# Keys and values compressed side by side in the array, compressed scores in one pass, and value products gathered into one run

## The chip, the cores and the metric

The kernel runs on one core of a Trainium2 chip. The metric is the device time of one execution in microseconds. Three runs of the kernel before gave 1069.88, 1070.99 and 1071.37, a median of 1070.99.

## What is computed

The input is one sequence of 512 tokens, 1024 wide. The first block is an RMS norm, one wide projection, a sliding-window attention (8 heads, 2 key heads, window 128), a short gated convolution, an output projection and a gated feed-forward net of width 2816. The second block projects again and mixes three things. One is a sparse attention of 6 heads in 2 groups with three branches (compressed, selected and window) that share their queries; the others are a stick-breaking attention (4 heads) and a gated recurrence (6 heads). The parts of the reference that the change touches, cut:

```python
def compress(src, w1, w2):
    blocks = src.reshape(B, S, G, dk)[:, blk_idx] + cmp_pos[None, None, :, None, :]
    blocks = blocks.transpose(0, 3, 1, 2, 4).reshape(B, G, n_cmp, CMP_BLOCK * dk)
    return jax.nn.gelu(blocks @ w1) @ w2
kc = compress(kc_src, w_ck1, w_ck2)
vc = compress(vc_src, w_cv1, w_cv2)
...
s_c = jnp.einsum('bghtd,bgnd->bghtn', qb, kc) * scale + bias_c
p_c = masked_softmax(s_c, rel_c >= 0)
o_c = jnp.einsum('bghtn,bgnd->bghtd', p_c.astype(vc.dtype), vc)
...
return gb[..., 0:1] * o_c + gb[..., 1:2] * o_s + gb[..., 2:3] * o_w
```

Here `n_cmp` is 31 blocks per group, so 62 for both groups; a block has 32 tokens of width 64, that is 2048 numbers, or 16 slices of 128. With 512 tokens the selected branch sees every earlier block, so it is a full causal attention.

## The kernel before, in words

**Dense products.** Activations stand as 128 channels by 512 tokens. Every weight block of 1024 x 128 comes by one DMA into `raw` (2 buffers), is split into a rounded part `wh` (ScalarE, L196) and a rest `wl` (VectorE, L136 from L197), and gives 24 matmuls of 512 columns in `dense` (8 slices, three products each). The product ends in a PSUM bank (`pm`, two banks; the first four blocks of a stage alternate with `poa` and `pob`), and VectorE reads the bank (`dk<-pm,rs` and the like). Those matmuls use the type fp32r, and each is one record in the trace. A matmul of plain fp32 operands is two records there.

**The second block.** `in_proj2` goes through 33 weight blocks in the order of the table ORDER: `kc` is the third, `vc` the sixth, and the eight gates `z` end it. Beside it run three generators: `stream_a` (recurrence pairs and stick-breaking pairs, in the order of SEQ), `sparse` (the compressed branch, then 24 units of the other two branches) and `finishing`. `drive` writes them out by costs that each yields, divided by rates, and a scheduler that orders by priority and readiness makes the instruction order of each engine from that.

**The compressed branch.** `compress` (L840) is run for the keys and then for the values. It loads `w_ck1` or `w_cv1` (4 DMAs of 256 KB into `nk` buffers) and a small second weight, builds 62 blocks with VectorE adds (L857) and makes 16 fp32 matmuls (the weight slice stands still, 62 columns move), then a chain of eight small ScalarE and VectorE steps for the GELU. Small products follow: the keys `kcT` (128 x 62) and the values `vcn`. For each of 4 token blocks `compressed` then makes the scores: for each of two groups three fp32 matmuls with the query block standing still and 31 key columns moving, `pgb<-kcT,np`.

**The value products.** A unit of the sparse part (head pair j, token block i, branch br) makes scores (`nsa_a`), a softmax, transposes of the probabilities (L965), a copy of them to SBUF by VectorE for one group and ScalarE for the other (`pT`, L967), and products with the values (`pob<-nk,np`). Each product uses half the array's columns, since a group has 64 of the 128 output rows; the two groups alternate. `run` puts the products of one unit together at high priority, and they wait for the copies. The products of the compressed branch (`pob<-np,vcn`) go with branch 0. The first block's `softmax_b` works alike: 8 units, each with one run into `poa` or `pob`.

## Time and profile before

| what | value |
|---|---|
| median of 3 runs | 1070.99 us |
| the profiled execution, its own time | 1068.53 us |
| its span in the trace | 1066.8 us |
| granted TensorE clock, mean | 0.999 of 2.4 GHz |
| TensorE (PE) busy | 1039.5 us, 97% |
| VectorE (DVE) busy | 704.4 us, 66% |
| ScalarE (ACT) busy | 488.8 us, 46% |
| GpSimd (POOL) busy | 44.0 us, 4% |
| DMA | 97.84 MB, mean 92 GB/s |

The span is what the instructions cover, and 1.7 us of the execution lie around it. Busy time of PE is a modelled figure: matmuls overlap, so two records of 0.39 us can start 0.23 us apart. What a matmul costs is therefore read from where the next one starts.

### The profile page before, as it was taken

How to read it: one execution, taken by the hardware profiler on the slowest of the kernel's cores; microseconds unless marked ns; L12 is line 12 of the kernel's file. 1: busy time of each engine (PE TensorE's matmuls, PEld its weight loads, DVE VectorE, ACT ScalarE, POOL GpSimd, SP SyncE). 2: the span in 40 equal slices, each digit the busy share in tenths (PEclk: the TensorE clock that was granted, in tenths of full speed). 3: DMA queues.
4: the chain of work that ended last, by engine and by line, in shares of the span. 5: the costliest groups of instructions: out<-in, count | busy, mean ns of one | idle time of the engine just before them, and what ended most of it. 6: DMA issues, size and time to landing. Idle time of an engine off the chain costs nothing.

```text
span 1066.8 us, 14636 instructions
## 1 busy us (share of the span) xinstructions
PE 1039.5 (97%) x5712; PEld 838.9 (79%) x5712; DVE 704.4 (66%) x1313; ACT 488.8 (46%) x855; POOL 44.0 (4%) x89
## 2 busy tenths in 40 slices
PE   8999999999999999999999999999999999989997
PEld 6788888888888888888877888767777777767886
DVE  6876643356448777777763233597967698887757
ACT  5754443322344444444442222433625676578740
POOL 0000000000220000000000111200000000011000
PEclk9999999999999999999999999999999999999999
DMA  6212232333432233223335333531321110101232
GB/s 218 79 60 80 79 94 85 99 99 109 142 120 85 98 99 99 98 99 99 99 94 193 97 106 90 184 101 41 99 75 47 59 41 22 41 21 37 82 120 79
DMA packets 32801, 97.84 MB, mean 92 GB/s; under 512 B 4878, under 2 KB 5390, under 8 KB 32732
## 3 DMA queue, kind: packets, MB, share of 16 engines
q1 hardware_dynamic: 32732, 96.91, 28.7%
q8 instruction: 45, 0.74, 0.3%
q14 instruction: 24, 0.20, 0.1%
HBM read 94.77 MB, written 5.27 MB: 94 GB/s over the span
## 4 chain that ended last, share of the span: by engine, by line
PE 75%; DVE 11%; ACT 7%; DMA 3%; issue 2%; SPq 1%; POOL 1%; DVEq 0%; POOLq 0%; ACTq 0%
PE pm L139 44%; PE pob L139 12%; PE poa L139 12%; PE pga L139 4%; PE pgb L139 3%; DVE wl L136 2%; DMA raw<-in_w_in 1%; ACT wh L196 1%; DVE lv L136 1%; DMA raw<-in_w_down 1%; DVE hk L136 1%; DVE dk L136 1%; DVE np L136 1%; DVE nk L942 1%; ACT nk L948 1%
## 5 line engine op out<-in xcount | busy, mean ns | idle before, releaser
L139 PE MATMUL pm<-x,wh 128*128 128x512 f32 (+1 forms) x1360 | 433.4, 395 | 2.1 <-DVE x L133 0.9
L139 PEld LDWEIGHTS pm<-x,wh 128*128 128x128 f32 (+1 forms) x1360 | 252.2, 187 | 58.5 <-issue 3.5
L196 ACT CAST wh<-raw 128x1024 fp32r<-128x1024 f32 (+1 forms) x153 | 156.7, 1025 | 275.8 <-issue 109.9
L139 PE MATMUL pm<-x,wl 128*128 128x512 f32 (+1 forms) x680 | 268.3, 395 | 0.0
L136 DVE TENSOR_TENSOR wl<-raw,wh 128x1024 fp32r<-128x1024 f32 (+1 forms) x153 | 181.9, 1189 | 89.5 <-ACT wh L196 87.7
L139 PEld LDWEIGHTS pm<-x,wl 128*128 128x128 f32 (+1 forms) x680 | 127.0, 187 | 26.8 <-issue 1.6
L139 PE MATMUL poa<-x,wh 128*128 128x512 f32 x208 | 65.0, 394 | 0.0
L139 PE MATMUL pob<-x,wh 128*128 128x512 f32 x208 | 64.1, 390 | 0.0
L139 PE MATMUL pm<-np,wh 128*128 128x512 f32 x176 | 54.1, 389 | 0.0
L136 DVE TENSOR_TENSOR dk<-pm,rs 128x512 f32<-128x512 f32 x43 | 29.5, 686 | 28.1 <-PE pm L139 28.0
L139 PEld LDWEIGHTS poa<-x,wh 128*128 128x128 f32 x208 | 39.0, 188 | 9.3 <-issue 1.0
L139 PEld LDWEIGHTS pob<-x,wh 128*128 128x128 f32 x208 | 39.0, 188 | 8.0
L136 DVE TENSOR_TENSOR nk<-pm,rs 128x512 f32<-128x512 f32 x34 | 23.4, 687 | 32.6 <-PE pm L139 32.4
L139 PE MATMUL poa<-x,wl 128*128 128x512 f32 x104 | 40.6, 390 | 0.1
L139 PE MATMUL pob<-x,wl 128*128 128x512 f32 x104 | 40.6, 390 | 0.0
L139 PEld LDWEIGHTS pm<-np,wh 128*128 128x128 f32 x176 | 33.0, 188 | 6.8
L139 PE MATMUL pm<-np,wl 128*128 128x512 f32 x88 | 34.2, 389 | 0.0
L948 ACT ACTIVATE nk<-nk,q 128x128 f32<-128x128 f32 (+3 forms) x48 | 26.5, 555 | 11.5 <-DVE q L946 11.2
L942 DVE CUSTOM_DVE_ANT_0 nk<-pgb,bi 128x128 f32<-128x128 f32 (+3 forms) x48 | 23.1, 484 | 7.9 <-PE pgb L139 7.2
L133 DVE SCALAR_TENSOR_TENSOR dk<-nk,smt,dk 128x511 f32<-128x511 f32 (+1 forms) x34 | 25.4, 748 | 1.4 <-ACT dk L435 0.8
L139 PE MATMUL pgb<-np,np 128*128 128x128 f32 (+3 forms) x96 | 25.9, 351 | 0.4 <-DVE nk L967 0.3
L133 DVE SCALAR_TENSOR_TENSOR nk<-nk,smt,nk 128x511 f32<-128x511 f32 (+2 forms) x33 | 24.7, 747 | 0.5
(498 smaller groups left out, 1664.7 us busy)
## 6 DMA issues: line engine op xcount, KB each, us to landing
raw<-in_w_in SPq DMA_DIRECT2D x65, 512.0 KB, 3.5
raw<-in_w_up SPq DMA_DIRECT2D x44, 512.0 KB, 3.5
raw<-in_w_down SPq DMA_DIRECT2D x16, 512.0 KB, 3.6
raw<-in_w_br SPq DMA_DIRECT2D x8, 512.0 KB, 3.4
raw<-in_w_out SPq DMA_DIRECT2D x8, 512.0 KB, 3.5
raw<-in_w_out SPq DMA_DIRECT2D x16, 256.0 KB, 2.7
raw<-in_w_down SPq DMA_DIRECT2D x8, 384.0 KB, 3.2
d<-d SPq DMA_DIRECT2D x6, 512.0 KB, 6.6
```

The costliest lines, as they stand in the source:

```text
L133: V.scalar_tensor_tensor(o, i0, s, i1, op0, op1)
L136: V.tensor_tensor(o, i0, i1, op)
L139: return TE.matmul(o, l, r, start=start, stop=stop)
L196: A.copy(wh[:, c], raw[:, c])
L942: V.tensor_tensor_reduce(pb[:, 0:Wd_], s[:, 0:Wd_], bias[h][:, T - Wd_:T], 1.0, -3e38, ALU.add, ALU.max, st[:, g:g + 1])
L948: A.activation(pbs[g][:, 0:Wd_], pbs[g][:, 0:Wd_], AF.Exp, bias=st[:, 2 + g:3 + g], accum_out=st[:, 4 + g:5 + g])
```

## The change

Four things are changed.

1. `compress` becomes `blocks`, which only loads weights and builds blocks, for keys and then for values, and `compressed` makes the products of both together. The blocks now stand still (64 columns at a time, two of them unused) and the weights move (128 columns). Keys write output rows 0 to 63 and values 64 to 127 of one bank, 32 fp32 products in one `run`. The GELU chain is made once, 128 x 128, and one transpose turns its result. The `w1` tiles, blocks and the chain come from `np` in place of `nk` buffers, and both values' and keys' loads are issued ahead.
2. The keys are kept as a rounded part and a rest side by side (`kc2`, 62 columns, fp32r). The scores of a token block are 6 fp32r products of 62 columns into one bank, and VectorE adds the two halves and the bias.
3. `nsa_b` keeps its transposes and copies, and `nsa_c` makes the products of both branches of a token block in one run. In the first block `softmax_c` does so for the two units of a head pair.
4. Buffers move: the probabilities of the first block to `lv`, some gates from `lv` to `hk` and `np`, three merged tiles from `np` to `lv`.

```diff
     def small(w):
-        return qp.tile([P, w], F32, tag=f"q{w}", name=nm("q"), bufs={6: 1, 8: 4, 20: 4, 32: 2, 192: 2, 64: 5}.get(w, 6))
+        return qp.tile([P, w], F32, tag=f"q{w}", name=nm("q"), bufs={6: 1, 8: 4, 20: 4, 32: 2, 192: 2, 64: 2}.get(w, 6))
...
                 j = n - 18
                 t = scaled(ps, rstd1)
-                g = tl("bi" if j < 6 else "lv" if j < 12 else "hk" if j < 15 else "np")
+                g = tl("bi" if j < 6 else "hk" if j < 9 else "np")
...
-    def softmax_b(j, ip, po, sbs, lo):
...
-            pT = wk()
+            pT = tl("lv")
             c = slice(lo[0], T)
...
@@ -508,28 +516,33 @@
             i = 2 * ip + u
             bs = list(range(lo[u] // P, 2))
             for b in bs:
-                sblk = i + b - 1
                 for hh in range(2):
-                    r = 64 * hh
-                    todo.append(later(po[r:r + 64, i * P:(i + 1) * P], vn[:, sblk * P + r:sblk * P + r + 64],
-                                      pts[hh][:, (2 * u + b) * P:(2 * u + b + 1) * P], b == bs[0], b == bs[-1]))
-        run(todo, ends)
-        yield 1.0
+                    todo.append((i, i + b - 1, hh, pts[hh][:, (2 * u + b) * P:(2 * u + b + 1) * P], b == bs[0], b == bs[-1]))
+        return todo, ends
+
+    def softmax_c(po, held):
+        todo = []
+        for i, sblk, hh, w, first, last in held[0][0] + held[1][0]:
+            r = 64 * hh
+            todo.append(later(po[r:r + 64, i * P:(i + 1) * P], vn[:, sblk * P + r:sblk * P + r + 64], w, first, last))
+        run(todo, held[0][1] + held[1][1])
+        yield 2.0
...
             new = softmax_a(*un) if un else None
             yield 1.7
             if prev:
                 (j, ip), args = prev
-                if ip == 0:
+                held.append((yield from softmax_b(j, ip, *args)))
+                if ip == 1:
                     po = bank("oa" if j % 2 == 0 else "ob")
-                yield from softmax_b(j, ip, po, *args)
-                if ip == 1:
+                    yield from softmax_c(po, held)
+                    held = []
                     attn[j] = split(po, None, rt)
...
-            merged[j] = split(ms[0], 0.5, of("np" if j < 5 else "gp"))
...
-    def compress(name, w1name, w2name):
-        w1 = [nk().rearrange("p (k h) -> p k h", k=4) for _ in range(4)]
+    def blocks(name, w1name, w2name):
+
+        w1 = [np_().rearrange("p (k h) -> p k h", k=4) for _ in range(4)]
         for n in range(4):
             nc.sync.dma_start(w1[n], a[w1name][:, 4 * n:4 * n + 4])
         w2 = small(64)
         nc.sync.dma_start(w2, a[w2name])
         yield from need(name)
         src = pr[name]
-        blks = [nk(), nk()]
+        blks = [np_(), np_()]
         pos = S("pos").rearrange("p (r j) -> p r j", r=2)
         for n in range(2):
+            G.memset(blks[n][:, 496:512], 0.0)
             blk = blks[n][:, 0:496].rearrange("p (j n) -> p j n", j=8)
             for g in range(2):
                 s = src[64 * g:64 * g + 64]
                 for par in range(2):
                     v = bass.AP(tensor=s.tensor, offset=s.offset + par + 16 * n,
                                 ap=[list(s.ap[0]), [2, 8], [16, 31]])
-                    V.tensor_tensor(
+                    last = V.tensor_tensor(
                         blk[64 * par:64 * par + 64, :, 31 * g:31 * g + 31], v,
                         pos[64 * g:64 * g + 64, par, 8 * n:8 * n + 8].unsqueeze(2).to_broadcast([64, 8, 31]), ALU.add,
                     )
         yield 0
-        ps = bank("gb")
-        for k in range(16):
-            mm(ps[:, 0:62], w1[k // 4][:, k % 4], blks[k // 8][:, 62 * (k % 8):62 * (k % 8) + 62], k == 0, k == 15)
-        x, y = small(64), small(64)
-        A.copy(x[:, :62], ps[:, 0:62])
-        tt(y[:, :62], x[:, :62], x[:, :62], ALU.mult)
-        V.tensor_scalar(y[:, :62], y[:, :62], 0.044715, 1.0, ALU.mult, ALU.add)
-        tt(y[:, :62], y[:, :62], x[:, :62], ALU.mult)
-        V.tensor_scalar(y[:, :62], y[:, :62], -2.0 * math.sqrt(2.0 / math.pi), 80.0, ALU.mult, ALU.min)
-        A.activation(y[:, :62], y[:, :62], AF.Exp)
-        V.tensor_scalar(y[:, :62], y[:, :62], 1.0, None, ALU.add)
-        V.reciprocal(y[:, :62], y[:, :62])
-        tt(y[:, :62], y[:, :62], x[:, :62], ALU.mult)
-        pr[w1name] = y, w2
-        yield 2.0
-
-    kcT = cp.tile([P, 2, 32], F32, tag="kcT", name="kcT")
+        return w1, w2, blks, last
+
+
+    kc2 = cp.tile([P, 2, 64], F32R, tag="kc2", name="kc2")
     vcn = [cp.tile([P, 2, 64], F32, tag=f"vcn{h}", name=f"vcn{h}") for h in range(3)]
...
-        yield from compress("kc", "w_ck1", "w_ck2")
-        y, w2 = pr["w_ck1"]
+        wk1, wk2, bk, e0 = yield from blocks("kc", "w_ck1", "w_ck2")
+        wv1, wv2, bv, e1 = yield from blocks("vc", "w_cv1", "w_cv2")
+
+        ps = bank("gb")
+        todo = []
+        for k in range(16):
+            c = slice(62 * (k % 8), 62 * (k % 8) + 64)
+            for r, w1, blks in ((0, wk1, bk), (64, wv1, bv)):
+                todo.append(later(ps[r:r + 64, 0:P], blks[k // 8][:, c], w1[k // 4][:, k % 4], k == 0, k == 15))
+        run(todo, [e0, e1])
+        xy = np_()
+        x, y, yT = (xy[:, P * n:P * n + P] for n in range(3))
+        A.copy(x, ps[:, 0:P])
+        tt(y, x, x, ALU.mult)
+        V.tensor_scalar(y, y, 0.044715, 1.0, ALU.mult, ALU.add)
+        tt(y, y, x, ALU.mult)
+        V.tensor_scalar(y, y, -2.0 * math.sqrt(2.0 / math.pi), 80.0, ALU.mult, ALU.min)
+        A.activation(y, y, AF.Exp)
+        V.tensor_scalar(y, y, 1.0, None, ALU.add)
+        V.reciprocal(y, y)
+        tt(y, y, x, ALU.mult)
+        yield 2.0
+        ps = bank("gb")
+        TE.transpose(ps[:, 0:P], y, ident)
+        A.copy(yT, ps[:, 0:P])
         ps = bank("gb")
         for g in range(2):
             for r in (0, 64):
-                mm(ps[r:r + 64, 32 * g:32 * g + 31], w2, y[:, 31 * g:31 * g + 31])
-        A.copy(kcT[:, :, 0:31], ps[:, 0:64].rearrange("p (g n) -> p g n", g=2)[:, :, 0:31])
+                mm(ps[r:r + 64, 32 * g:32 * g + 31], wk2, yT[:, 31 * g:31 * g + 31])
+        kv = ps[:, 0:64].rearrange("p (g n) -> p g n", g=2)[:, :, 0:31]
+        A.copy(kc2[:, :, 0:31], kv)
+        tt(kc2[:, :, 31:62], kv, kc2[:, :, 0:31].bitcast(F32), ALU.subtract)
         yield 0.3
-        yield from compress("vc", "w_cv1", "w_cv2")
-        y, w2 = pr["w_cv1"]
         ps = bank("gb")
         for g in range(2):
             for h in range(3):
-                mm(ps[32 * h:32 * h + 31, 64 * g:64 * g + 64], y[:, 31 * g:31 * g + 31], w2)
+                mm(ps[32 * h:32 * h + 31, 64 * g:64 * g + 64], yT[:, 64 + 31 * g:64 + 31 * g + 31], wv2)
         for h in range(3):
             A.copy(vcn[h][32 * h:32 * h + 31], ps[32 * h:32 * h + 31, 0:128])
         yield 0.5
...
             pv = pc.rearrange("p (h n) -> p h n", n=32)[:, :, 0:31]
             st = small(16)
+            ps = bank("gb")
             for g in range(2):
-                ps = bank("gb")
                 for h in range(3):
-                    mm(ps[:, 32 * h:32 * h + 31], pr["nq", h][g][:, i * P:(i + 1) * P].bitcast(F32), kcT[:, g, 0:31])
-                tt(pv[:, 3 * g:3 * g + 3], ps[:, 0:96].rearrange("p (h n) -> p h n", n=32)[:, :, 0:31],
-                   biasc[i][:, 3 * g:3 * g + 3], ALU.add)
+                    n = 64 * (3 * g + h)
+                    mm(ps[:, n:n + 62], pr["nq", h][g][:, i * P:(i + 1) * P], kc2[:, g, 0:62])
+            sv = ps[:, 0:384].rearrange("p (h n) -> p h n", h=6)
+            tt(pv, sv[:, :, 0:31], biasc[i], ALU.add)
+            tt(pv, pv, sv[:, :, 31:62], ALU.add)
...
-    def nsa_b(j, i, br, po, pbs):
+    def nsa_b(j, i, br, pbs):
+
         Wd_ = (i + 1) * P
-        vn_ = pr[("vs", "vw")[br]]
         pts, ends = [], []
         for g in range(2):
             ps = bank("gb")
@@ -967,24 +994,31 @@
             ends.append((V.tensor_copy if g == 0 else A.copy)(pT[:, 0:Wd_], ps[:, 0:Wd_]))
             pts.append(pT)
         yield 0.25 * (i + 1)
-        todo = []
+        return pts, ends
+
+    def nsa_c(j, i, po, held):
+
+        todo, ends = [], []
         for g in range(2):
-            if br == 0:
-                todo.append(later(po[64 * g:64 * g + 64, i * P:(i + 1) * P], vcn[j][0:96, g],
-                                  pcT[i][0:96, g], True, False))
-        for b in range(i + 1):
-            for g in range(2):
-                r = 64 * g
-                todo.append(later(po[r:r + 64, i * P:(i + 1) * P], vn_[:, b * P + r:b * P + r + 64],
-                                  pts[g][:, b * P:(b + 1) * P], False, br == 1 and b == i))
+            todo.append(later(po[64 * g:64 * g + 64, i * P:(i + 1) * P], vcn[j][0:96, g],
+                              pcT[i][0:96, g], True, False))
+        for br, (pts, e) in enumerate(held):
+            vn_ = pr[("vs", "vw")[br]]
+            ends += e
+            for b in range(i + 1):
+                for g in range(2):
+                    r = 64 * g
+                    todo.append(later(po[r:r + 64, i * P:(i + 1) * P], vn_[:, b * P + r:b * P + r + 64],
+                                      pts[g][:, b * P:(b + 1) * P], False, br == 1 and b == i))
         run(todo, ends)
-        yield 0.16 * (i + 1)
+        yield 0.32 * (i + 1)
...
-                yield from paced(nsa_b(j, i, br, po, pbs), rate)
+                held.append((yield from paced2(nsa_b(j, i, br, pbs), rate)))
+                if br == 1:
+                    yield from paced(nsa_c(j, i, po, held), rate)
+                    held = []
```

Three places show how the order of the instructions moves. All are on PE. First the products of the compression: the keys' before, in `pgb_5297`, where `x4` is four matmuls of one weight tile (`pob_5341` is the dense product they interrupt).

```order
L139 MATMUL pob_5341<-x_4698,wh_5257 128x512
L139 MATMUL pgb_5297<-nk_5287,nk_5151 128x62 x4
L139 MATMUL pgb_5297<-nk_5287,nk_5152 128x62 x4
L139 MATMUL pob_5341<-x_4697,wl_5258 128x512
L139 MATMUL pob_5341<-x_4790,wh_5257 128x512
```

And now, where keys (`np_5151` and on) and values (`np_5299` and on) alternate in `pgb_5680`, behind the value products of a recurrence pair (`poa_5548`):

```order
L139 MATMUL poa_5548<-hk_5537,gp_5342 64x128
L139 MATMUL pgb_5680<-np_5300,np_5668 64x128
L139 MATMUL pgb_5680<-np_5152,np_5287 64x128
L139 MATMUL pgb_5680<-np_5300,np_5668 64x128
L139 MATMUL pgb_5680<-np_5152,np_5287 64x128
L139 MATMUL pgb_5680<-np_5300,np_5668 64x128
L139 MATMUL pgb_5680<-np_5153,np_5288 64x128
L139 MATMUL pgb_5680<-np_5301,np_5669 64x128
```

Four pieces of eight matmuls, each among full-array work, became 32 matmuls in three pieces (6, 5 and 21) with 64 output rows each; the last two stand on either side of that recurrence run.

Second, the value products of head pair 0, token block 1, in the first of its two branches, before (`vcn` is the compressed branch, `np_6029` the values of the selected one):

```order
L139 MATMUL pm_7730<-x_4790,wl_7415 128x512
L139 MATMUL pob_6661<-np_6550,vcn_5082 64x128 x2
L139 MATMUL pob_6661<-nk_6664,np_6029 64x128
L139 MATMUL pob_6661<-nk_6668,np_6029 64x128
L139 MATMUL pgb_6680<-np_5987,np_5782 128x256
L139 MATMUL pgb_6680<-np_5989,np_5782 128x256
```

And now, with the window branch's products (`np_6429`) in the same run:

```order
L139 MATMUL pm_7776<-x_5059,wl_7456 128x512
L139 MATMUL pob_6652<-np_6544,vcn_5082 64x128 x2
L139 MATMUL pob_6652<-nk_6655,np_6024 64x128
L139 MATMUL pob_6652<-nk_6659,np_6024 64x128
L139 MATMUL pob_6652<-nk_6681,np_6429 64x128
L139 MATMUL pob_6652<-nk_6685,np_6429 64x128
L139 MATMUL pgb_6694<-np_5936,np_5776 128x256
```

The second run of the pair is gone as a piece of its own. Counted over the whole order, stretches of matmuls on 64 output columns went from 37 to 22, and stretches on the full array from 51 to 34.

Third, the end of the last dense block that comes before six gate blocks are left. Before, from its last row on (`pm_8245`), 84 matmuls stand ahead of the next dense one:

```order
L139 MATMUL pm_8245<-x_5059,wl_8170 128x512
L139 MATMUL pob_7783<-nk_7849,np_6434 64x128
L139 MATMUL pob_7783<-nk_7853,np_6434 64x128
L139 MATMUL pgb_7869<-np_5942,np_5903 128x256
L139 MATMUL pgb_7869<-np_5944,np_5903 128x256
```

Now the same block (`pm_8266`) ends while head pair 1 is in work, and the third recurrence pair (`lv_7558`) comes behind it:

```order
L139 MATMUL pm_8266<-x_5059,wl_8195 128x512
L992 MATMUL pgb_7400<-cst,nk_7120 128x128 x4
L992 MATMUL pgb_7407<-cst,nk_7125 128x128 x4
L139 MATMUL pgb_7474<-np_5936,np_5897 128x128
L139 MATMUL pgb_7474<-np_5938,np_5897 128x128
```

284 matmuls now stand ahead of the next dense one, all of the third recurrence pair's products among them. Before, that pair stood ahead of the dense block's end.

## Rows read from the trace of the kernel before

**Rows 1.** The page: busy time, share of the span, instructions.
```profile
PE 1039.5 (97%) x5712; PEld 838.9 (79%) x5712; DVE 704.4 (66%) x1313; ACT 488.8 (46%) x855; POOL 44.0 (4%) x89
```

**Rows 2.** Timeline of PE at the keys' compression: start, us, engine, line, tiles, records.
```profile
700.01 2.00 PE L139 MATMUL pgb<-nk,nk 128*128 128x62 f32 x16 [0.35 <-DVE nk L857]
701.82 0.71 PE L139 MATMUL pob<-x,wh 128*128 128x512 f32 x2
```

**Rows 3.** Timeline of PE, two runs of value products and their neighbours.
```profile
941.56 0.40 PE L139 MATMUL pm<-x,wl 128*128 128x512 f32 x1
941.88 0.44 PE L139 MATMUL pob<-nk,np 128*64 128x128 f32 x4
942.25 0.50 PE L139 MATMUL pgb<-np,np 128*128 128x256 f32 x2
...
983.68 0.39 PE L139 MATMUL pm<-x,wl 128*128 128x512 f32 x1
983.91 0.39 PE L139 MATMUL pm<-x,wh 128*128 128x512 f32 x1
984.23 0.44 PE L139 MATMUL pob<-np,vcn 96*64 96x128 f32 x4
984.50 1.05 PE L139 MATMUL pob<-nk,np 128*64 128x128 f32 x16
985.47 0.50 PE L139 MATMUL pm<-x,wh 128*128 128x512 f32 x1
```

**Rows 4.** Waits of PE from 679 to 740 us: total, times, longest.
```profile
PE pgb L139 <- DVE nk L857: 1.3, 2, 1.0
PE pgb L139 <- issue: 0.8, 1, 0.8
```

**Rows 5.** Timeline of PE at the compressed scores, and fp32r products of 128 columns.
```profile
840.07 0.75 PE L139 MATMUL pgb<-kcT,np 128*128 128x31 f32 x6
840.66 0.71 PE L139 MATMUL pm<-x,wh 128*128 128x512 f32 x2
...
1009.92 0.61 PE L139 MATMUL pga<-trir,x 128*128 128x128 f32 x4
1010.37 0.39 PE L139 MATMUL poa<-trir,x 128*128 128x128 f32 x2
```

**Rows 6.** Waits of PE from 895 to 1005 us, the longest one.
```profile
PE pob L139 <- ACT nk L967: 1.6, 3, 0.8
```

**Rows 7.** Chain that ended last, 640 to 760 us: start, us, what.
```profile
658.60 14.74 PE pob L139 x65
673.45 6.29 DMA raw<-in_w_in
...
680.91 1.23 DVE wl L136
```

**Rows 8.** Timeline of PE, the first product of that third block.
```profile
686.28 0.62 PE L139 MATMUL pm<-x,wh 128*128 128x512 f32 x2
```

**Rows 9.** Timeline of SP: the loads ahead of that block and behind it.
```profile
670.65 2.70 SPq L821 DMA_DIRECT2D bi<-d  x6
...
676.12 2.26 SPq L843 DMA_DIRECT2D nk<-in_w_ck  x4
```

**Rows 10.** Busy time in stretches: us; PE, PEld, DVE, ACT, POOL; clock; DMA.
```profile
869.20:907.70 38.50, 37.97 (x422) 29.28 (x423) 34.34 (x114) 24.97 (x67) 1.61 (x5) 1.00 0.07 21
907.70:959.70 52.00, 48.23 (x384) 35.28 (x382) 43.56 (x138) 32.34 (x84) 2.70 (x6) 1.00 0.10 31
959.70:1008.60 48.90, 47.11 (x286) 37.63 (x286) 36.90 (x62) 39.43 (x70) 4.34 (x11) 1.00 0.17 50
```

**Rows 11.** Timeline of DVE: two reads of dense banks, one after the other.
```profile
908.00 0.68 DVE L136 TENSOR_TENSOR dk<-pm,rs 128x512 f32<-128x512 f32 x1
...
959.99 0.68 DVE L136 TENSOR_TENSOR dk<-pm,rs 128x512 f32<-128x512 f32 x1
```

**Rows 12.** Busy time in the stretch without dense work, columns as above.
```profile
941.30:960.50 19.20, 15.79 (x107) 10.69 (x105) 16.94 (x55) 14.92 (x39) 3.46 (x8) 1.00 0.09 28
```

More of the change, by code (lines that the diff above doesn't have):

```diff
@@ L162, in paced, with paced2 @@
         for c in g:
+            yield c if c is None else c / rate
+    def paced2(g, rate):
+        while True:
+            try:
+                c = next(g)
+            except StopIteration as e:
+                return e.value
             yield c if c is None else c / rate
@@ L491, in softmax_a, with softmax_b @@
         return sbs, lo
-    def softmax_b(j, ip, po, sbs, lo):
+    def softmax_b(j, ip, sbs, lo):
         pts, ends = [], []
@@ L521, in attention @@
         units = [(j, ip) for j in range(4) for ip in range(2)]
-        po = None
+        held = []
         prev = None
@@ L557, in branches @@
             tt(ms[0], ms[0], ms[1], ALU.add)
-            merged[j] = split(ms[0], 0.5, of("np" if j < 5 else "gp"))
+            merged[j] = split(ms[0], 0.5, of("np" if j < 2 else "lv" if j < 5 else "gp"))
     drive((branches(), 1.0))
@@ L680, in tile_net @@
     A.copy(trir[:, 2], ident)
-    dk, hk, nk = of("dk"), of("hk"), of("nk")
+    dk, hk, nk, np_ = of("dk"), of("hk"), of("nk"), of("np")
     def pairs(t):
@@ L987, in sparse @@
         po = None
+        held = []
         for un in [(j, i, br) for j in range(3) for i in range(4) for br in range(2)] + [None]:
@@ L995, in sparse @@
                     po = bank("ob")
-                yield from paced(nsa_b(j, i, br, po, pbs), rate)
+                held.append((yield from paced2(nsa_b(j, i, br, pbs), rate)))
+                if br == 1:
+                    yield from paced(nsa_c(j, i, po, held), rate)
+                    held = []
                 if (i, br) == (3, 1):
```

## The prediction

> **What bounds the kernel now.** I began with the page's busy times. TensorE is busy 97% of the span, VectorE 66% and ScalarE 46% [rows 1]. So a matmul saved is worth its own time, as long as the engine then finds other work. Two more views are needed. The timeline of PE, read from one start to the next, prices the matmuls that change [rows 2, 3, 5]: the reader should divide the distance to the next row's start by the number of records, since the lengths printed overlap. The busy times of stretches show where PE is not the limit. From 869 to 1009 us it has 133.3 us of work in 139.4 us (the three stretches summed), while VectorE and ScalarE have 114.8 and 96.7 [rows 10]. In the one long stretch without dense products, 941.3 to 960.5, PE is busy 15.8 of 19.2 us and VectorE 16.9 [rows 12]. There a saved matmul is not yet a saved microsecond.
>
> **The change part by part.** The sum is made against the profiled execution's own time, 1068.53 us, which is 2.5 us under the median of the runs.
>
> *Compression.* Before, the keys' first eight products are 16 records from 700.01 to 701.82, 0.113 us each [rows 2]. Both compressions have 64 records, so 7.2 us. After, there are 32 products, again 64 records, on half the columns and with 128 columns moving. The trace has that form in the value products. A run of 4 records takes 0.37 us to the next start and one of 20 records 1.24 [rows 3], so 16 more records cost 0.87, or 0.054 each. 64 of them are 3.5 us: a saving of **3.7**. It needs the two halves to work at the same time; if they didn't, a record would cost about what the full array's does, and the saving would be 0.
>
> *Waits at the compression.* Four pieces among full-array work waited 2.1 us on the block adds L857 and on issue [rows 4]. The adds remain, but one gathered run behind a recurrence run, further back in the order, needs them. I take **1.0** saved, between 0 and 2.1. The extra transpose is one record, 0.1 us more. The GELU chain is made once in place of twice. In the order 29 dense products, 6.6 us, stand between it and the transpose. That hides its eight steps of 128 columns even at the 0.68 us that 512 columns take on VectorE, 5.4 us [rows 11]; without them all of that would show.
>
> *Scores.* Six records take 0.59 us [rows 5], and there are eight such groups, 4.7 us. After, there are 24 fp32r products of 62 columns, which the trace does not show. The nearest row is fp32r with 128 columns, four records in 0.45 us, 0.11 each [rows 5], that is 2.6 us. The upper bound is two records of 0.11, 5.3 us, which would cost 0.6; the lower is half the nearest row, 1.3 us. I take 0.11, the nearest row, and a saving of **2.1** (-0.6 to 3.4). VectorE's eight adds of bias become eight of twice the width; dense work lies beside them.
>
> *Gathered runs.* A run on half columns costs something at its ends. Into it, the start of the next matmul comes 0.32 us after a 512-column one in place of 0.23, and the run of 4 records takes 0.37 where 4 times 0.054 are 0.21 [rows 3]. Together that is 0.25 us per run. The order has 37 stretches of this kind before and 22 after, 4 fewer in the first block, 12 fewer in the sparse part and one more for the compression. 15 times 0.25 gives **3.8**, with bounds of 3 and 4.5. A run also waits for the copies of the probabilities, 1.6 us in three visible waits [rows 6]. Half as many runs wait, but each for the later of two branches' copies: I take **0.5**, between 0 and 1.6.
>
> *Loads.* SP issues in order. Before, the four `w_ck1` loads left at 676.1, behind the table of biases (670.7) and the third weight block, issued at 673.45 [rows 7, 9]. Now they and two of `w_cv1`, 1.5 MB, stand ahead of the biases, two of them ahead of the second weight block. They wait for `np` buffers that the last product of the feed-forward net reads as slices 8 to 16 of 22, so from about 664 to 670 in its 14.7 us from 658.6 [rows 7]. Before, biases and third block, 2 MB, took 9.1 us from 670.65 to 679.7, and 1.5 MB are 6.8 us at that pace. Some 5 of them fit ahead of the biases. The block's split ended at 682.1 and its first product came at 686.3, 4.1 us of slack [rows 7, 8], so that some 2 us of lateness would not show. I take 0.5 us lost, between 0 and 3.
>
> *The stretch without dense work.* This term is the least sure. VectorE reads one dense bank at 908.0 and the next at 960.0 [rows 11]; in the order 136 of its instructions lie from one read to the other, now 176. In the stretch ahead (from 869.2) they go from 112 to 83, in the one behind (to 1008.6) from 61 to 49, so that the total stays (309 and 308). Before, one was busy 0.316 us on average there (43.56 us for 138 [rows 10]); 176 are 55.6 us. At the share of before, 84%, the middle takes 66 us, 14 more. The first part falls by some 6: its 210 matmuls need 32 us at the spacings above. The last falls by some 8: 138 dense products at 0.23 are 32 us, the rest 9. I take **0**. The ends are 10 us gained (VectorE never idle in the middle) and 8 lost (VectorE at 75%, its share in the last stretch of rows 10).
>
> The sum is -3.7 - 1.0 + 0.1 - 2.1 - 3.8 - 0.5 + 0.5 + 0 = **-10.5 us**: 1058.0 for the profiled execution, 1060.5 for the median. Moving buffers in the first block I cost at nothing: the gates wait for no one there, dense products lie beside them, and if a gate waited for its buffer VectorE would hold up a bank for one block, 5.4 us at most.
>
> **The rivals.** *VectorE sets the middle stretch.* For it: 284 matmuls now stand without a dense one where 84 did, with the recurrence and two sparse head pairs asking for VectorE at once. Against it: two independent chains fill each other's waits. The middle then takes 70 to 74 us in place of 66, and 4 to 8 of the 10.5 are given back: 1064.5 to 1068.5.
>
> *The halves don't work at once.* The row says they do: 0.054 us a record against 0.113 on the full array [rows 2, 3], but there each half has its own values and probabilities in a run of at most 20 records. Without it the compression saves nothing and the sum is -6.8, 1064.2. The Trainium skill, TensorE: Matmul & The Clock Gate, section "Part 3: Packing small matmuls — row/col tiling", has a weight load overlap a running matmul only where the row group differs, and here all products use all rows. By that rule the loads would stand between the products and this rival would hold; the trace disagrees, since the value products come at 0.054 us.
>
> *The scores keep two records.* If the product of 62 columns cost what fp32 did, the change would not do what it says there: the sum is -7.8, 1063.2. Against it: every fp32r matmul in the trace is one record.
>
> *The weight blocks come late.* If none of the 1.5 MB is through before the biases leave, the third block is 6.8 us late, 2.7 more than its slack, and the 0.5 of the sum becomes 2.7: 1062.7. For it: the buffers come free one after the other, and the second weight block stands behind two of them.
>
> *Slower than before.* The middle stretch is the place again, with ScalarE and VectorE waiting for each other down one chain: recurrence, then stick-breaking, then the gate blocks that wait for its `dk` buffers. It decides when VectorE's share there falls under 72%: 55.6 us of work then take 77 us, 11 more than the forecast. At 65% it is 85.5 us, and the median 1080. Against it: the share was 84% with fewer chains, and 88% without dense work [rows 12].
>
> **How the numbers follow.** The forecast gets 0.61, VectorE in the middle 0.19, the halves 0.05, the scores 0.05, the late weights 0.05 and slower 0.05. All but the last are faster by over 0.2% (2.1 us, about what a measurement of this kernel can tell from no change), except the upper edge of the second, which I give 0.04, and half of the last, 0.02, which ends within 0.2%. So faster 0.91, same 0.06, slower 0.03. The forecast's own terms range from about -16 (waits at their good ends, -2.2, and a third of the gain in the middle, -3.3) to -7 (waits, loads and scores at their bad ends). The range goes from 1054.5 to 1068: it takes in those bounds, and all rivals but the slower one and the edge.
>
> **What would show it.** In the profile of the changed kernel, `pgb<-np,np 64x128` should stand at 0.054 us a record, 64 of them; `pgb<-kc,np` at one record each, 0.11 us; 12 runs into `pob` and one run per head pair in the first block, each with its entry of 0.32 us. The stretch from the last dense product before the six gate blocks to the next should take 40 to 45 us, the middle between the two reads of VectorE about 66. The forecast is wrong if that middle takes over 74 us, if PE waits for `wh` or `wl` near 685 us, or if the compression's records are 0.1 us apart.

## The result, and the profile after

The changed kernel takes 1080.63 us (four runs, 1078.16 to 1082.20), the kernel before 1070.76: a ratio of 1.0098 with a 95% interval of 1.0084 to 1.0112. It is slower, by 9.9 us, where 10.5 less were forecast. Its profiled execution took 1078.16 us, 9.6 more than that of before.

The page, busy times and granted clock in 40 slices; against [rows 1] little has moved:
```profile
PE 1038.7 (96%) x5689; PEld 841.3 (78%) x5689; DVE 705.2 (66%) x1307; ACT 488.1 (45%) x854; POOL 45.9 (4%) x93
...
PEclk9999999999999999999999999999999999789999
```
TensorE has as much busy time as before, although 23 records are gone. The second line gives a reason: in two of the 40 slices (35 and 36, 915 to 969 us) the granted clock was well under full, which it was in no slice before (0.999 in the mean, now 0.989).

To see where the time went I counted the 512-column products on weight blocks in both traces (3576 each, 24 to a block) and noted when the same product starts, from the first weight block's end on (there the changed kernel is 0.5 us ahead). Blocks are counted from 0, and a stretch begins and ends at the last product of the block named. The table gives what each stretch gained or lost, in us:

| stretch (weight blocks) | forecast | after |
|---|---|---|
| first block's attention (1 to 30) | -1.0 | -1.4 |
| feed-forward net and its start (30 to 116) | 0 | -0.7 |
| loads (116 to 118) | +0.5 | +0.5 |
| compression (118 to 129) | -4.4 | +0.4 |
| scores, sparse part, middle (129 to 148) | -5.6 | +11.5 |
| end | 0 | -0.2 |

Two stretches failed, and they failed in waits, not in the price of a matmul. The timeline of PE in the changed kernel:
```profile
677.84 1.12 PE L139 MATMUL pgb<-nk,ones 128*128 128x512 f32 x2 [1.37 <-POOL nk L302]
...
699.42 0.66 PE L385 MATMUL pga<-cst,dk 128*128 128x128 f32 x4 [2.71 <-DVE dk L136]
699.83 0.71 PE L139 MATMUL pm<-x,wh 128*18 128x512 f32 x2
700.38 0.40 PE L139 MATMUL pm<-x,wl 128*18 128x512 f32 x1
...
726.07 0.88 PE L139 MATMUL pgb<-np,np 128*64 128x128 f32 x12 [1.10 <-ACT hk L1222]
726.88 0.71 PE L139 MATMUL pga<-lv 64*128 64x128 f32 x8
727.52 0.87 PE L139 MATMUL pgb<-np,np 128*64 128x128 f32 x10
728.38 2.40 PE L139 MATMUL poa<-hk,gp 128*64 128x128 f32 x40
730.61 2.57 PE L139 MATMUL pgb<-np,np 128*64 128x128 f32 x42
733.11 1.12 PE L139 MATMUL pga<-hk,cst 128*128 128x512 f32 x2
...
830.99 0.83 PE L139 MATMUL pgb<-kc,np 128*128 128x62 f32 x6
831.66 0.36 PE L139 MATMUL pga<-gp,np 128*128 128x256 f32 x1
...
916.51 0.45 PE L139 MATMUL pm<-x,wl 128*128 128x512 f32 x1
918.56 1.09 PE L992 MATMUL pgb<-cst,nk 128*128 128x128 f32 x8 [1.61 <-DVE nk L982]
...
921.10 3.63 PE L139 MATMUL pob<-nk,np 128*64 128x128 f32 x32
924.66 0.69 PE L139 MATMUL pgb<-np,np 128*128 128x128 f32 x2
...
975.13 0.73 PE L139 MATMUL pm<-x,wh 128*128 128x512 f32 x2
...
981.33 1.92 PE L139 MATMUL pob<-nk,np 128*64 128x128 f32 x32
983.17 0.44 PE L139 MATMUL pga<-hk,trir 128*128 128x384 f32 x1
```
The 64 records of the compression stand in three pieces, 0.81, 0.86 and 2.50 us to the next start: 0.065 each, entries included, against 0.113 in [rows 2]. Six scores take 0.67 us, 0.11 each, as taken from [rows 5]. But no dense product starts between 916.51 and 975.13, 58.6 us, where the stretch of [rows 12] had 19. And in it a run of 32 records takes 3.56 us to the next start; a run of the same form takes 1.84 at 981.33, where the clock was full.

The windows of the changed kernel (columns as in [rows 10]: busy time of PE, PEld, DVE, ACT, POOL; then the granted clock):
```profile
893.58:974.40 80.82, 69.75 (x606) 53.25 (x605) 57.80 (x179) 40.26 (x108) 2.91 (x8) 0.87 0.06 21
916.90:975.10 58.20, 46.98 (x450) 35.92 (x449) 41.74 (x121) 30.86 (x80) 2.91 (x8) 0.82 0.03 10
...
915.00:930.00 15.00, 12.88 (x210) 10.58 (x208) 10.41 (x35) 6.02 (x17) 0.00 (x0) 0.77 0.11 36
930.00:945.00 15.00, 11.00 (x71) 7.65 (x70) 11.78 (x39) 4.88 (x17) 0.00 (x0) 0.77 0.00 1
...
960.00:975.00 15.00, 13.42 (x77) 10.45 (x77) 9.95 (x24) 10.58 (x25) 2.25 (x7) 0.77 0.00 1
```
VectorE's timeline has the two reads of dense banks that bound the first window:
```profile
893.58 0.68 DVE L136 TENSOR_TENSOR dk<-pm,rs 128x512 f32<-128x512 f32 x1
...
974.40 0.68 DVE L136 TENSOR_TENSOR dk<-pm,rs 128x512 f32<-128x512 f32 x1
```
The stretch between these reads was 52.0 us in [rows 11] and is now 80.8. VectorE does there what was counted (179 instructions and 57.8 us; 176 and 55.6 were forecast), but it is busy 72% of it and not 84%. The clock of 0.82 in the long stretch is a mixture of the two levels: 0.50 of 2.4 GHz in three pieces of 6.8 to 6.9 us (from 919.5, 933.2 and 960.5 us on), each at the end of a wait of PE or just behind it, and full in between.

PE's waits in the two stretches (690 to 760, and 918 to 975 us): total, times, longest:
```profile
PE pga L385 <- DVE dk L136: 2.7, 1, 2.7
PE pga L139 <- DVE hk L1211: 1.4, 1, 1.4
PE pm L139 <- DVE dk L133: 1.3, 1, 1.3
PE pgb L139 <- ACT hk L1222: 1.1, 1, 1.1
...
PE pgb L139 <- DVE nk L994: 3.1, 4, 1.9
PE pga L139 <- ACT hk L1076: 2.5, 1, 2.5
PE pgb L992 <- DVE nk L982: 1.8, 2, 1.6
```
The first four, 6.5 us, are new at the compression; those of [rows 4], 2.1 us, are gone. VectorE's timeline at the longest:
```profile
695.12 2.92 DVE L872 TENSOR_TENSOR np<-nk,smt 64x248 f32<-64x248 f32 x5
698.08 0.69 DVE L136 TENSOR_TENSOR hk<-gp 128x512 f32<-128x512 f32 x1
698.69 0.68 DVE L136 TENSOR_TENSOR dk<-pob,rs 128x512 f32<-128x512 f32 x1
```
The read of the bank that the transposes at 699.42 need stands behind five block adds (2.92 us) and a step of the recurrence. VectorE is busy 29.8 of the 30 us from 690 to 720 there; it was 28.8 before. PE comes to this place sooner, since the keys' products are no longer here, and then waits.

### The profile page after: what moved, and what is told of

The parts are those of the page before. It is cut to its first block, busy times and chain, and to the rows that moved or that the text cites. A ratio compares the mean times of both kernels' runs of the same rounds, so it can differ in the third digit from the quotient of the medians.

```text
span 1076.5 us, 14582 instructions
## 1 busy us (share of the span) xinstructions
PE 1038.7 (96%) x5689; PEld 841.3 (78%) x5689; DVE 705.2 (66%) x1307; ACT 488.1 (45%) x854; POOL 45.9 (4%) x93
## 4 chain that ended last, share of the span: by engine, by line
PE 75%; DVE 12%; ACT 8%; DMA 2%; issue 2%; POOL 1%; SPq 1%; POOLq 0%; DVEq 0%; ACTq 0%
PE pm L139 43%; PE pob L139 12%; PE poa L139 12%; PE pga L139 3%; PE pgb L139 3%; DVE wl L136 2%; DVE hk L136 1%; DVE lv L136 1%; ACT wh L204 1%; ACT nk L975 1%; DVE dk L136 1%; DMA raw<-in_w_down 1%; DVE dk L133 1%; DVE np L136 1%; PE pgb L992 1%
## 5 line engine op out<-in xcount | busy, mean ns | idle before, releaser
L139 PE MATMUL pm<-np,wh 128*128 128x512 f32 x152 | 46.8, 389 | 0.0
L136 DVE TENSOR_TENSOR dk<-pm,rs 128x512 f32<-128x512 f32 x42 | 28.8, 686 | 23.3 <-PE pm L139 23.2
L139 PE MATMUL pgb<-np,np 128*64 128x128 f32 (+4 forms) x160 | 30.6, 329 | 4.9 <-DVE nk L994 2.8
L139 PEld LDWEIGHTS pm<-np,wh 128*128 128x128 f32 x152 | 28.5, 188 | 6.0
L139 PEld LDWEIGHTS pgb<-np,np 128*128 128x128 f32 (+1 forms) x160 | 20.1, 176 | 13.1 <-DVE nk L994 4.2
L139 PE MATMUL pm<-np,wl 128*128 128x512 f32 x76 | 29.6, 389 | 0.0
L133 DVE SCALAR_TENSOR_TENSOR nk<-nk,smt,nk 128x511 f32<-128x511 f32 (+2 forms) x33 | 24.7, 747 | 1.3 <-ACT nk L443 0.8
```

The costliest lines, as they stand in the source:

```text
L133: V.scalar_tensor_tensor(o, i0, s, i1, op0, op1)
L136: V.tensor_tensor(o, i0, i1, op)
L139: return TE.matmul(o, l, r, start=start, stop=stop)
```

## The experiments

The theories: the instruction order that the planner (`drive` and the scheduler behind it) makes from the costs (**order**); probabilities held longer for a gathered run (**buffers**); VectorE at the compression (**VectorE**); the half clock behind waits (**clock**). All are compared with the kernel before on the same chip, 1068.9 to 1069.1 us there.

**1 and 2: the planner's cost.** The change drops a cost with the second compression: two of `yield 2.0` became one.

```diff
         tt(y, y, x, ALU.mult)
-        yield 2.0
+        yield 4.0
```


> The changed kernel with one number changed: the step that ends the compression tells the planner a cost of 4.0 in place of 2.0, as the two compressions before told together. No instruction is added or removed. Order theory (the lower cost brought the sparse work about 6 us of planned time forward, which left the third recurrence pair, the second stick-breaking pair and two sparse head pairs without dense products beside them): the stretch of 284 matmuls without a dense one falls to 82, the 16 us that were lost from 900 to 990 us come back, the granted clock there is 1.00 again, and the time is 1060 to 1065 us. Buffer theory (four probability tiles held for a gathered run keep the sparse chain waiting): 1076 us or more, since the tiles are held as before. VectorE theory (it has too much work in the middle whatever the order): 1074 us or more.

The second puts the lower total into the kernel before:
```diff
         pr[w1name] = y, w2
-        yield 2.0
+        yield 1.0
```


> The kernel before with one number changed: each of its two compressions tells the planner 1.0 in place of 2.0, so that the total is 2.0 lower, as in the changed kernel. Nothing else of the change is in it. Order theory: in its instruction order a stretch of 75 and one of 190 matmuls follow each other with almost no dense product between them, so it loses 10 to 20 us: 1081 to 1091 us, with a lower granted clock in the middle. Buffer theory and the theory that gathered runs are the cause: 1069 to 1073 us, no change.

Measured: 1069.08 us for the first (ratio 0.9997, 0.9983 to 1.0011, where the changed kernel has 1.0098); 1084.10 for the second (1.0132, 1.0114 to 1.0150), 15 over the kernel before, from a number that adds no instruction. VectorE's reads of two dense banks, one after the other, in the first:
```profile
903.88 0.68 DVE L136 TENSOR_TENSOR dk<-pm,rs 128x512 f32<-128x512 f32 x1
957.50 0.68 DVE L136 TENSOR_TENSOR dk<-pm,rs 128x512 f32<-128x512 f32 x1
```
and in the second:
```profile
900.64 0.69 DVE L136 TENSOR_TENSOR dk<-pm,rs 128x512 f32<-128x512 f32 x1 [0.98 <-PE pm L139]
978.50 0.68 DVE L136 TENSOR_TENSOR dk<-pm,rs 128x512 f32<-128x512 f32 x1
```
53.6 and 77.9 us, against 52.0 before and 80.8 after. The order theory holds: the middle is lost by the cost alone, and neither held buffers nor gathered runs are needed for it. But the first run is 4 us over its range, and its clock was not full in the middle as expected (half from 945.7 to 949.1 and from 955.9 to 959.3 us). Its 12 executions spread from 1064.57 us at a mean clock of 0.995 to 1072.17 at 0.986, 0.8 us per thousandth, and its timeline of PE shows why:
```profile
699.89 1.12 PE L385 MATMUL pga<-cst,dk 128*128 128x128 f32 x4 [2.71 <-DVE dk L136]
700.66 1.20 PE L139 MATMUL pm<-x,wh 128*18 128x512 f32 x2
701.66 0.63 PE L139 MATMUL pm<-x,wl 128*18 128x512 f32 x1
```
It is the wait of the changed kernel to the hundredth, but here the products behind it stand 0.77 and 1.00 us apart where it was 0.41 and 0.55: the granted clock was half from 699.9 to 703.3 us, and full at this place in the changed kernel's profile. The Trainium skill, TensorE: Matmul & The Clock Gate, "Part 1: The HAM clock gate", has the low clock as the default that activity lifts. These rows agree, with the addition that an equal wait costs the clock in one execution and not in another.

**3, 4 and 5: one part undone.** On the first run's kernel: old compressions (3), sparse value products per branch (4), both (5). The core of each:
```diff
-        wk1, wk2, bk, e0 = yield from blocks("kc", "w_ck1", "w_ck2")
-        wv1, wv2, bv, e1 = yield from blocks("vc", "w_cv1", "w_cv2")
+        yield from compress("kc", "w_ck1", "w_ck2")
...
-                held.append((yield from paced2(nsa_b(j, i, br, pbs), rate)))
-                if br == 1:
-                    yield from paced(nsa_c(j, i, po, held), rate)
+                yield from paced(nsa_b(j, i, br, po, pbs), rate)
```


> The kernel of the first run with the two old compressions, one after the other on the full array, in place of the joint one (scores, gathered runs and buffers of the change stay). The prediction's price: 64 records at 0.113 against 0.054 us and 1.0 of waits, so 4.7 us slower than the first run. VectorE theory (from 690 to 725 us VectorE is busy without a break in both kernels and PE waits for it, so a matmul saved there only becomes a wait): at most 1.5 us slower than the first run.

> The kernel of the first run with the value products of the sparse part written out per branch as before: 12 more half-column runs, and no tiles held from one branch to the next. The prediction's price: 12 times 0.25 us and 0.5 of waits, 3.5 us slower than the first run. Theory that a gathered run gives this back by waiting for both branches' copies: within 1 us of the first run. Buffer theory: faster than the first run.

> The kernel of the first run (cost 4.0) with both the old compressions and the value products of the sparse part per branch as before; what is left of the change is the scores in one pass, the gathered runs of the first block and the buffers. Against the third run it undoes the gathered runs alone. The prediction's price of a gathered run: 3.5 us slower than the third run (1067). Theory that a gathered run, in this instruction order, gives back in the middle what it saves: 1060 to 1064, at or under the third run. Against the fourth run it undoes the joint compression alone: 4.7 us slower by the prediction's price, within 1.5 us by the VectorE theory.

Measured: 1063.37 (0.9944, 0.9927 to 0.9961), 1063.55 (0.9941, 0.9924 to 0.9958) and **1061.17 us** (0.9921, 0.9904 to 0.9938), with 1060.64 to 1061.93 in six runs. Undoing a part makes it faster, by 5.5 us and more, which no theory's range had for the third and only the buffer theory for the fourth. With the runs ungathered, the joint compression costs 2.4 us (4 against 5), outside the 1.5 that the VectorE theory allowed. Its 3 us of records come to nothing, as that theory says; the mean clock was 0.995 against 0.998 in the median, and at 0.8 us a thousandth that is an estimate of 2.4 us. The gathered runs cost 2.2 us (3 against 5). By the count of dense products, blocks 129 to 148 gain 3.3 us with gathered runs (3) and 5.3 without (5). Their waits of PE, 860 to 1010 us, in the third:
```profile
PE pga L139 <- ACT hk L1066: 2.3, 3, 1.1
PE pga L139 <- DVE hk L136: 0.9, 3, 0.5
PE pga L139 <- DVE lv L136: 0.7, 2, 0.4
```
and in the fourth:
```profile
PE poa L139 <- POOL hk L1035: 1.3, 1, 1.3
PE pob L139 <- ACT nk L994: 1.0, 3, 0.4
```
The longest waits of the third are those of stick-breaking for its chain (L1066), and the fourth and fifth have none of 0.2 us or more. In the third's order scores stand there in doubles; in the fifth's a branch's products stand between them. But the kernel before has 1.4 us of the same wait without gathering, so gathering alone does not make it. Whether the held tiles or the planner put them so was not separated.

**6, 7 and 9: the keys' adds on GpSimd**, on the kernels of runs 1, 4 and 5:
```diff
-                    last = V.tensor_tensor(
+                    last = (G if name == "kc" else V).tensor_tensor(
```


> The kernel of the first run with the eight block adds of the keys on GpSimd in place of VectorE. VectorE theory: the read of the next dense bank and the recurrence's steps no longer stand behind 4.7 us of adds, PE's wait of 2.9 us near 697 us goes and with it the half clock that followed it; 2 to 6 us faster than the first run (1063 to 1067) and less spread. If the wait of 2.9 us stays or moves to GpSimd's adds, the theory is wrong: 1068 to 1070, no change.

> The joint compression with the keys' block adds on GpSimd, the value products of the sparse part per branch, cost 4.0: the parts that each run so far speaks for. VectorE theory: faster than the fourth run by 2 to 4 us, 1059 to 1062, the fastest so far. Otherwise as the fourth run, 1063.

> The kernel of the fifth run with the eight block adds of the keys on GpSimd. VectorE theory: PE's waits at the old compression, 2.1 us in the kernel before, stand behind the adds on VectorE too, so some 1 to 2 us faster than the fifth run, 1059 to 1060, and the fastest of all. If GpSimd's adds take longer than VectorE's and the compression waits for them, 1061 or more.

Measured: 1064.68 (4.4 less than run 1), 1061.72 (1.8 less than run 4) and 1069.16 us (8.0 more than run 5). The ranges of the sixth and seventh held (the seventh was not the fastest), but the row that was to show the sixth's cause does not: the wait of 2.9 us is still there.
```profile
699.67 1.11 PE L385 MATMUL pga<-cst,dk 128*128 128x128 f32 x4 [2.95 <-DVE dk L136]
```
Other steps of the recurrence took the place of the adds ahead of that read. And while GpSimd's adds ran (690.93 to 699.59 us) VectorE's steps took longer; its timeline there:
```profile
695.19 2.96 DVE L136 TENSOR_TENSOR hk<-gp 128x512 f32<-128x512 f32 x3
```
One such step took 0.69 us in the changed kernel (698.08 above), so three end to end would take some 1.9. With three other steps in that time VectorE lost 2.4 us by the same comparison, most of the wait that stayed. So the row doesn't tell whether the adds alone held the read back before. What went is the waits further on (1.5, 1.3 and 1.1 us in run 1, on L1211, L133 and L1222), and the order had moved with the edit: the 64 records of the compression stand in one piece.
```profile
727.92 3.71 PE L139 MATMUL pgb<-np,np 128*64 128x128 f32 x64 [0.16 <-issue]
```
Which part of the 4.4 us is the adds and which the order was not separated. The ninth shows the price: GpSimd and then PE:
```profile
691.63 7.79 POOL L870 TENSOR_TENSOR nk<-nk,smt 64x248 f32<-64x248 f32 x8 [12.31 <-DVE nk L136]
...
695.92 3.00 PE L139 MATMUL pgb<-nk,nk 128*128 128x62 f32 x16 [3.28 <-POOL nk L870]
```
An add takes 0.97 us there and 0.58 on VectorE. The old compression needs them at once and waits 3.28 us, and its 16 records are busy 3.00 us where [rows 2] has 2.00: the clock fell again behind the wait (half from 696.7 to 706.9 us). The joint one of run 6 does not start before 727.9 us, well behind them.

**8: the scores alone.** Run 5 with the old scores, so that only the first block's runs and the buffers are left of the change.
```diff
-                    mm(ps[:, n:n + 62], pr["nq", h][g][:, i * P:(i + 1) * P], kc2[:, g, 0:62])
+                    mm(ps[:, 32 * h:32 * h + 31], pr["nq", h][g][:, i * P:(i + 1) * P].bitcast(F32), kcT[:, g, 0:31])
```


> The kernel of the fifth run with the old scores (48 fp32 records in eight groups, each group with a bank of its own): what is left of the change is the gathered runs of the first block and the moved buffers. The prediction's prices: the scores 2.1 us (so 1063.3, 2.1 over the fifth run) and four runs at 0.25 us (so 1.0 under the kernel before, 1068). If the scores are worth more than their records, because one bank per token block in place of two lets the dense products run on, it is 4 us or more over the fifth run.

Measured: 1067.55 us (0.9986, 0.9972 to 1.0000). The first block's runs and the buffers are worth 1.3 us, near the 1.0 forecast, with an interval that reaches from 0 to 3.0. The scores are worth 6.4, three times their records. The two profiled executions are 9.3 us apart. In the count of dense products 5.3 of these lie in blocks 129 to 148, where run 8 equals the kernel before and has its waits on stick-breaking too, and 3.4 at the compression, where the clock of run 8's execution fell to half (727.6 to 734.5 us). Why the scores move the middle was not tried further.

**10, 11 and 12: work in the waits.** Products whose result nobody reads, ahead of transposes that overwrite their bank: 12 on runs 1 and 7, of which 9 stand at the wait of 2.7 us and 3 at 572 us; 40 in the changed kernel, 35 of them in the long stretch.
```diff
     def to_nat(src, dst, tag="ga", fill=0):
         ps = bank(tag)
+        for _ in range(fill):
+            mm(ps, trir[:, 2], x2[0][0])
```


> The kernel of the first run with 12 dense-sized products more, whose result nobody reads: they write the bank that the next transposes overwrite, and in the order 9 of them stand where PE waited 2.9 us near 697 us, 3 earlier (0.7 us of added work). Clock theory (the half clock of 5 us behind that wait comes from PE's idleness in it): the granted clock from 698 to 706 us stays at 1.00, PE no longer idles there, and the transposes start when they did; the median falls by 0.5 to 2 us, to 1067 to 1068.5. If the clock falls there as before, or the products push the transposes back, the median rises by 1 to 3 us.

> The kernel of the seventh run with the same 12 products. Clock theory: the runs at a mean clock of 0.992 to 0.995 (1061.7 to 1063.5 us) go over to those at 0.998 (1059.5), so a median of 1060 to 1061. Otherwise 1061.7 to 1064.5.

> The changed kernel itself (cost 2.0, the stretch of 284 matmuls without a dense one) with 40 products of 512 columns more in that stretch and right behind it, whose result nobody reads: for each sparse unit from the last one of head pair 1 on, up to 4 stand ahead of the first transposes of its probabilities, in the bank that these overwrite. That is 9 us of added work. Clock theory (most of what the long stretch loses, about 8 us, is the half clock that PE's waits bring, at 0.84 us for each thousandth of the mean clock as the first run's executions show): the granted clock from 915 to 990 us stays nearer 1.00 than the 0.89 before, and the time does not rise although 9 us of work are added: 1074 to 1080 us. Chain theory (the stretch is as long as the chain through VectorE and ScalarE, and the clock is a bystander): the products that stand ahead of the transposes push the chain back, 1082 to 1089 us, or fit into the waits, 1080 to 1082.

Measured: 1065.67 (3.4 less than run 1, with 12 products more), 1061.52 (as run 7; its spread falls from 4.1 to 1.8 us) and 1080.17 us (1.0092, 1.0069 to 1.0115, where the changed kernel has 1.0098, with 40 products more). The tenth fell by more than its range, the eleventh lies between its two. In run 10, on the timeline of PE:
```profile
695.84 2.26 PE L139 MATMUL pga<-x,trir 128*128 128x512 f32 x9
700.13 0.66 PE L387 MATMUL pga<-cst,dk 128*128 128x128 f32 x4 [2.03 <-DVE dk L136]
```
The nine are through before the wait ends, 2.03 us remain, and in this execution the clock still fell behind it. The median clock, 0.9945 against 0.991, is higher. But the order moved with the added products: the compression's 64 records stand in one piece, as in run 6, and the three waits of run 1 further on (3.9 us) are gone. So run 10 doesn't show that the clock made the 3.4 us. Run 7 has that one piece already, and there the same products are worth nothing measurable (run 11). In run 12 the windows that had 0.77 read:
```profile
915.00:930.00 15.00, 14.35 (x249) 11.68 (x247) 10.65 (x36) 5.97 (x16) 0.00 (x0) 1.00 0.10 36
930.00:945.00 15.00, 11.92 (x100) 8.79 (x94) 13.54 (x43) 5.45 (x18) 0.00 (x0) 1.00 0.01 1
...
960.00:975.00 15.00, 12.38 (x76) 9.51 (x77) 10.61 (x28) 10.54 (x25) 2.69 (x8) 0.89 0.01 2
```
The time from one dense product to the next is 54.7 us there in place of 58.6, with 35 added products in it and 11 records of the kernel's own fewer, and the half clock lasted 3.4 us in place of 20.5. So the clock is part of the loss, and not a bystander; the row at 921.10 above says so too, with 3.56 us for a run that takes 1.84 at full clock. Over blocks 129 to 148 the gain is 2.4 us, and in the profiled execution 2.8 more are lost at the compression than in the changed kernel's, since the clock fell twice there (from 701.3 and from 728.6 us). The total of 1080.17 lies where both theories' ranges meet, and the whole price of the clock can't be read from it.

## Why the prediction was wrong

- **Compression, 3.7.** The record's price held (0.065 against 0.054 us; the halves work at once, that rival is out). The saving is 64 times 0.048, 3.1 us, and it did not reach the end: the stretch lost 0.4. The step that failed is the sentence that a matmul saved is worth its own time "as long as the engine then finds other work": from 690 to 720 us VectorE has next to no idle time, and I looked for such a place only in the middle. That VectorE is what PE waits for there is read from the timelines; the runs that took its adds away (6 and 7) moved the order as well and don't show it alone.
- **Waits at the compression, 1.0.** Those went, 2.1 us, and 6.5 us of others came. The 29 dense products did cover the GELU chain: PE has no wait there.
- **Scores, 2.1.** Priced right by record; worth 6.4 in all (run 8). That rival is out too.
- **Gathered runs, 3.8 and 0.5 of waits.** Right in the first block (1.4 by the count, 1.3 by run 8). In the sparse part wrong in sign: 2.2 lost (run 5 against 3). I priced a run by its ends and not by the gaps that its products had filled.
- **Loads, 0.5.** Measured 0.5, but not by the weight blocks, whose rival is out: the block's first product at 684.28 waits for nothing. What waits is the norm at 677.84, 1.37 us for GpSimd's sum of squares, where the kernel before had 0.8.
- **The stretch without dense work, 0.** This is the step that decides: blocks 129 to 148 lost 11.5 where 5.6 were to be gained. The count of VectorE's work was right; its share, taken as that of before, was not. The sentence "two independent chains fill each other's waits" is what the runs refute. The slower rival named the place and the share (under 72%, measured 72%) and got 0.05. Its 1080 us fits by luck: it went with a share of 65%, and at 72% that rival has some 1071.5, since it kept the other terms, of which the compression's 4.4 failed as well. The order showed 284 matmuls without a dense one; I should have asked why they stood so. It was not the new work but a cost that the planner no longer saw (runs 1 and 2), and that could be read in the diff. The range had a slip beside this: with waits, loads and scores at their bad ends the sum is about -4, not -7, which the stated range still covers.
- **The clock** was in no term. Over 80 executions of the kernel before, shown beside these runs, a thousandth of mean clock goes with 0.78 us. The changed kernel has 0.988 in the median, the kernel before 0.997 in those 80: an estimate of 7 us of the 9.9, on top of the waits that bring it. It carries a slope from one kernel to another, and no run here shows the figure itself.

## What to carry to other kernels

Where an order is made from declared costs, a step that is merged or removed must leave its share of the planned time behind: restoring one number took the ratio from 1.0098 to 0.9997 here. When the order shows a long stretch without the work that fills waits, take the mean busy share of such stretches from the trace, not that of the mixed ones, and price the clock that idleness costs besides. The version to keep is run 5 (0.9921): the new scores and the first block's gathered runs, with the old compression and the old sparse runs. Run 7 has the same ratio with a wider spread. And an edit that a planner sees moves the order too, so that a gain is read beside the order and the waits further on.

## What was not expected of the hardware

Three steps of VectorE that take some 1.9 us end to end took 2.96 while GpSimd was adding (run 6). Products whose result is thrown away did not make a kernel slower: 40 of 512 columns left the time as it was (run 12), since they stood in waits and the clock fell for a shorter time. And one wait of 2.71 us, the same in two kernels, left the clock at full in one profile (the changed kernel) and halved it from 699.9 to 703.3 us in the other (run 1).
